# A shared ring of four SBUF slots split into two of two, and one product of the down projection read out by ACT

## The chip, the cores and the metric

The kernel runs on one core of a Trainium2 chip. Its engines are TensorE (PE, matrix products), VectorE (DVE), ScalarE (ACT), GpSimd (POOL) and SyncE (SP, which here issues most of the DMAs); each works through its own instructions in order and waits on semaphores for the others. SBUF is the working memory on the chip, PSUM receives PE's products. The metric is the device time of one execution in microseconds, as the median of the runs. Times in the trace are microseconds from the start of the span, durations marked ns are nanoseconds.

## What is computed

One layer of a post-norm trunk over 1024 positions of width 1024, in float32. A layer norm is followed by one input projection that feeds three mixers, an output projection, a norm, a gated feed-forward part with a gated input embedding, and a last norm:

```python
h = layer_norm(x, ln_in_g, ln_in_b)
proj = h @ w_in
a_q, a_f, a_i, a_g, b_u, b_v, c_q, c_kv, c_kr = split(proj)
o_a = hgrn2_mixer(a_q, a_f, a_i, a_g, ...)   # gated linear recurrence, 4 heads of 64
o_b = sgu_mixer(b_u, b_v, ...)               # causal gating in chunks of 128
o_c = mla_mixer(c_q, c_kv, c_kr, cos, sin, ...)   # causal attention, 8 heads, low-rank q and kv
mix = concatenate([o_a, o_b, o_c]) @ w_out
h = layer_norm(ALPHA * h + mix, ln1_g, ln1_b)
gate, up = split(h @ w_gate_up)
ffn = (silu(gate) * up) @ w_down             # D_FF = 2816
ple = sigmoid(h @ ple_w_gate) * (p @ ple_w_proj)
h = layer_norm(ALPHA * h + ffn + ple, ln2_g, ln2_b)
```

## The kernel before

Rows of positions lie in 8 tiles of 128. The projections take each float32 operand as a high and a low part and add three products (high by high, low by high, high by low), so one product of a 128-row tile with a weight of 1024 rows is 24 matmuls: `cq` 384 columns wide, `gb` 512, `ck` 288. In the trace a plain float32 matmul leaves two records.

The stages follow one another in time, by the trace: layer norm, embedding product and the value and gate projections of the recurrence (`vg`, products ai) to about 94 us; its forget and query projections (af, aq) to 138; the recurrence's scores in levels, to about 205; its chunk states (kE, kv); the low-rank query products (cq); from 237 the outputs of the recurrence (`ho`) and the gating unit (gb, uv, z), until 318; the key and value products (ck), the transposes ct and the q and k projections to 393; attention to 545; output projection, norm, embedding gate (pgt); the gate and up products from 725 to 1148; the down products to 1376; the last norm to the end.

**The recurrence's levels** (L420 to L447): the scores S of the recurrence are built in seven levels of two halves. For each half PE makes the products `lv` (L430) from q and k, DVE copies the masked part into S (L434) and multiplies q and k by the decay for the next level (L440, L443), which the next `lv` needs. Then, for four pairs of tiles (tp), a tile `vk` with the values is loaded from HBM (L464, L465), PE transposes k (kE, L470), ACT copies it (L473), PE makes kv from it and vk (L478), ACT copies that into kvs (L482), and DVE adds the states up (L485).

**cq** (L489 to L499): for each of the 8 tiles PE makes the product into a PSUM ring of two, ACT squares it into a tile `cn` (L495) to get the sum, POOL takes the inverse root (L140, L141), ACT scales the product into `cn` (L498), and SP stores `cn` to HBM (L499). ck (L565 to L574) does the same with its 8 tiles (L569, L572, L574). Later `cnl` loads them back, and PE transposes them (ct).

**ho** (L514 to L538): for each tp the values `vo` and gates `go` are loaded (L516, L518), PE makes the products of S with vo and of kvs with q into one PSUM tile (the only one of its ring), ACT squares it with sums (L533), POOL takes the inverse roots, DVE multiplies (L537, which is the last read of the PSUM tile) and multiplies by go (L538). The result is transposed (mx) and stored to `mix_d` (L458). The gating unit (L541 to L556) has its spatial weights and norm rows in a tile `sgp`, loaded at L503 to L507.

**gate and up** are Strassen-like products, seven of half-sized operands in place of eight; sums and differences of weights (`s`, on POOL at L1031 and elsewhere; `wp`, `st` on DVE at L110 and ACT at L790) are the operands. The last lines of such a product (L1008 to L1019) read the PSUM tiles.

**down** (L1093 to L1125) goes in two halves of chunks of the feed-forward width; `Down(i, ...)` holds the state of one block of rows i (0 to 3), and `product(m)` makes the seven products m. Their PSUM tiles dY, dZ, dW are opened by some m and reused by others with more terms; after each product its sum so far is added into the result tile r. Products 1, 7 and 6 go through an ACT copy into a tile `cp` (L1122) and a POOL add (L1123); the others are added by DVE straight from PSUM (L1125). In the last chunk the final norm of each row block runs beside the products (L1135 to L1157, L162, L163).

**Slots.** Every small tile comes from a ring with a fixed number of slots; a tile waits until the one that had its slot has been read for the last time. `ld` gives tiles of 128 x 512 words or less from the ring "X" with 4 slots, and `sm` is the same function under another name. From it come, in order of the program: vg (L277), the masks cmf and mski, `vk`, `cn` of cq, triu, vo and go, `cn` of ck, perm, the operands mixh and mixl, hx and sg at the embedding gate (L924, L935), g and s in gate, up and down (L1008, L1017, L1030), and four of every seven `cp`.

What sets the order on each engine is a scheduler: the program is written stage by stage, and the tile framework simulates it with its own durations and emits each engine's instructions in the order in which they came up there (`schedule_with_timeline_sim=True`). That order is then fixed: an engine never passes a waiting instruction. The number of slots of a ring thus changes the order on all engines.

Of the kernel before, what the change touches and what calls it, by code (L numbers as in the profile page):

```python
# [9 lines left out]
F32 = mybir.dt.float32  # L10
F32R = mybir.dt.float32r
# [3 lines left out]
ALU = mybir.AluOpType  # L15
AX = mybir.AxisListType

P = 128
# [25 lines left out]
def build(tc, A, out):  # L44
    nc = tc.nc
    ctx = ExitStack()
    with ctx:
# [9 lines left out]
        def nm(s):  # L57
            uid[0] += 1
            return f"{s}_{uid[0]}"
# [17 lines left out]
        smH = smt("smH", 3)  # L77

        def ld(shape, dt=F32, n="ld"):
            return xp.tile(list(shape), dt, tag="X", name=nm(n), bufs=4)  # L80

        sm = ld

        def ti(tag, w=8, bufs=4):
            return cp.tile([P, w], F32, tag="ti" + tag, name=nm("ti" + tag), bufs=bufs)
# [18 lines left out]
        V = nc.vector  # L104
# [597 lines left out]
        def mix_first():  # L702
            r = []
            for u in range(2):
                hi = ld([P, 4, P], F32R, n="mixh")
                lo = ld([P, 4, P], F32R, n="mixl")
                mr = lo.bitcast(F32)
                dma(out=mr, in_=mix_d[0][0][:, 4 * u:4 * u + 4])
                nc.scalar.copy(out=hi, in_=mr)
                sub_lo(V, lo, mr, hi)  # L710
                r.append((hi, lo))
            return [[r[k // 4][a][:, k % 4] for k in range(NK)] for a in range(2)]
# [94 lines left out]
        class Block:  # L807


            def __init__(self, n, new=None):  # L810
                self.t = [[(new or hb_tile)([P, 2, 512], n) for _ in range(2)] for _ in range(2)]
# [106 lines left out]
        for hf in range(2):  # L918
            wq = [wpage(A["w_pg"][hf * 4 + u]) for u in range(4)]
            cs = slice(hf * 512, hf * 512 + 512)  # L920
            for t in ((0, 1, 2, 3, 4, 5, 6, 7), (4, 5, 6, 7, 0, 1, 2, 3))[hf]:
                pl = t2("cp", 3, "pl")
                dma(out=pl, in_=pl_d[t][:, cs])
                hx = ld([P, 512], n="hx")  # L924
                dma(out=hx, in_=h1_d[t][:, cs])
                ps = ps_("ZYW"[n % 3], "pgt")
                c = slice((t % 4) * P, (t % 4 + 1) * P)
                for k in range(NK):
                    b = HB[k // 4, t // 4]
                    wh = wq[k // 2][0][:, (k % 2) * 512:(k % 2) * 512 + 512]  # L930
                    wl = wq[k // 2][1][:, (k % 2) * 512:(k % 2) * 512 + 512]
                    mm(ps, b.at(0, k % 4, c), wh, start=(k == 0), stop=False)  # L932
                    mm(ps, b.at(0, k % 4, c), wl, start=False, stop=False)  # L933
                    mm(ps, b.at(1, k % 4, c), wh, start=False, stop=(k == NK - 1))  # L934
                sg = ld([P, 512], n="sg")  # L935
                act(out=sg, in_=ps, func=AF.Sigmoid)
                V.tensor_tensor(out=sg, in0=pl, in1=sg, op=ALU.mult)
                V.scalar_tensor_tensor(out=sg, in0=hx, scalar=ALPHA, in1=sg, op0=ALU.mult, op1=ALU.add)
                dma(out=r_d[t][:, cs], in_=sg)
                n += 1  # L940
                if n in (3, 5, 11, 13):
                    sums_of_h((n - 3) // 2 if n < 9 else (n - 7) // 2)
# [78 lines left out]
        def down_operands(j, x0, x1):  # L1021

            a11, a21, a12, a22 = x0[:, :512], x0[:, 512:], x1[:, :512], x1[:, 512:]
            s = {1: a11, 2: a12, 4: a22}

            def step(m, in0=None, in1=None, how=None):
                def run():
                    if in0 is not None:
                        a, b = (s[q] if isinstance(q, int) else q for q in (in0, in1))
                        s[m] = ld([P, 512], n="s")  # L1030
                        G.tensor_tensor(out=s[m], in0=a, in1=b, op=how)  # L1031
                    st = (hb_tile([P, 2, 2, 256], "st") if j == NF // 2 - 1 else
                          gu.tile([P, 2, 2, 256], F32R, tag="st", name=nm("st"), bufs=2))
                    sv = s[m].rearrange("p (q n) -> p q n", q=2)
                    split(st[:, :, 0, :], st[:, :, 1, :], sv)
                    sdma(out=a_d[j][m].rearrange("q p a n -> p q a n"), in_=st.bitcast(F32))
                return run

            return [step(5, a21, a22, ALU.add), step(1), step(6, 5, a11, ALU.subtract), step(2),
                    step(3, a12, 6, ALU.subtract), step(4), step(7, a11, a21, ALU.subtract)]  # L1040
# [49 lines left out]
            return dn.tile([P, 512], F32, tag=tag, name=nm(n or tag), bufs=bufs)  # L1090

        class Down:
            def __init__(self, i, at, bt, opens):  # L1093
                self.i, self.at, self.bt, self.ps, self.opens = i, at, bt, {}, opens
                for t in (i, i + 4):
                    if r_t[t] is None:
                        r_t[t] = dn.tile([P, D], F32, tag="r", name=nm("r"), bufs=NT)

            def product(self, m):
                bank = BANK[m]  # L1100
                if m in OPENS:
                    self.ps[bank] = pd.tile([P, 512], F32, tag=bank, name=nm("d" + bank), bufs=DBUFS[bank])
                o = self.ps[bank]
                cs = slice((self.i % 2) * P, (self.i % 2 + 1) * P)
                a = self.at[self.i // 2][m]
                n = len(self.bt)
                for k in range(n):
                    b = self.bt[k][m]
                    mm(o, a[:, k, 0, cs], b[:, 0, :], start=(m in OPENS and k == 0), stop=False, skip_group_check=True)  # L1109
                    mm(o, a[:, k, 0, cs], b[:, 1, :], start=False, stop=False, skip_group_check=True)  # L1110
                    mm(o, a[:, k, 1, cs], b[:, 0, :], start=False, stop=(k == n - 1), skip_group_check=True)  # L1111
                r0, r1 = r_t[self.i], r_t[self.i + 4]
                r = {1: r0[:, :512], 2: r0[:, :512], 7: r1[:, 512:], 6: r1[:, :512], 4: r1[:, :512],
                     5: r1[:, 512:], 3: r0[:, 512:]}[m]
                if self.opens and m in (1, 7, 6):
                    nc.scalar.copy(out=r, in_=o)
                elif self.opens and m == 3:
                    V.tensor_copy(out=r, in_=o)
                elif m in (1, 7, 6):
                    nw[1] += 1  # L1120
                    c = ld([P, 512], n="cp") if nw[1] % 7 < 4 else d2("cp", 3)
                    nc.scalar.copy(out=c, in_=o)  # L1122
                    G.tensor_tensor(out=r, in0=r, in1=c, op=ALU.add)  # L1123
                else:
                    V.tensor_tensor(out=r, in0=r, in1=o, op=ALU.add)  # L1125

# [40 lines left out]
        for ci, js in enumerate(CHUNKS):  # L1167
# [19 lines left out]
                    dma(out=raw, in_=A["ln2"][u:u + 1, :].partition_broadcast(P))  # L1187
                    ln2.append(raw)
            for pair in ([(0, 1), (2,), (3,)] if last else [(0, 1), (2, 3)]):
                pair = [Down(i, at, bt, ci == 0) for i in pair]  # L1190
                for d in pair:
                    d.product(1)
                if pending:
# [101 lines left out]
```

## Time and profile before

| | us |
|---|---|
| median of 3 runs | 1397.91 (1396.21 to 1401.93) |
| profiled execution | 1394.26 |
| its span | 1392.5 |
| PE busy | 1313.4 (94%) |
| DVE busy | 937.2 (67%) |
| ACT busy | 593.4 (43%) |
| POOL busy | 572.6 (41%) |

The span runs from the first to the last instruction; 1.76 us of the profiled execution lie around it. An engine's busy time is an average over stages. PE is near its full span, so the stages where it is not are the ones to look at, by the table of busy time in stretches. In the timelines, the bracket at the end of a row gives the idle time of the engine just before the row, and the instruction that ended it. The mean granted clock of PE over the execution is 0.984.

### The profile page before, as it was taken

The numbers are of one execution on the slowest core, as the hardware profiler recorded it, in microseconds if no ns is written. First come the engines' busy times: TensorE is split into PE (matmuls) and PEld (weight loads), VectorE is DVE, ScalarE is ACT, GpSimd is POOL, SyncE is SP. The second block draws the span as 40 slices with busy tenths as digits, with TensorE's granted clock in tenths as the row PEclk, the third lists the DMA queues.
The fourth block names the chain that finished last, engine by engine and source line by source line (L and its number), as shares of the span: only waits on it lengthen the run. The fifth ranks groups of instructions, "written<-read, shape, count | busy, mean of one in ns | idle before, by whom it ended". The sixth has DMA issues, their size and how long they took to land.

```text
span 1392.5 us, 18446 instructions
## 1 busy us (share of the span) xinstructions
PE 1313.4 (94%) x6484; PEld 1097.4 (79%) x6484; DVE 937.2 (67%) x1357; ACT 593.4 (43%) x1189; POOL 572.6 (41%) x475
## 2 busy tenths in 40 slices
PE   6999779999989998999999999999999998999993
PEld 4788669898768887888888788888888876887882
DVE  7842691344567776676765787777777778577658
ACT  5543004335267775245434444444444445333441
POOL 3220002221223332323533554445544445899657
PEclk9999999999989999999999999999999999999997
DMA  9741002235595534447951444434434478996723
GB/s 328 260 137 46 31 1 90 90 96 160 157 336 121 113 72 150 163 179 262 314 191 61 165 159 148 145 139 145 157 137 152 166 265 308 393 316 228 258 61 121
DMA packets 105324, 237.52 MB, mean 171 GB/s; under 512 B 11152, under 2 KB 22416, under 8 KB 103696
## 3 DMA queue, kind: packets, MB, share of 16 engines
q1 hardware_dynamic: 84288, 195.97, 42.6%
q10 hardware_dynamic: 20944, 40.38, 7.7%
q8 instruction: 51, 0.84, 0.3%
q14 instruction: 41, 0.34, 0.1%
HBM read 150.98 MB, written 85.33 MB: 170 GB/s over the span
## 4 chain that ended last, share of the span: by engine, by line
PE 75%; DVE 9%; DMA 5%; POOL 4%; ACT 3%; issue 3%; SPq 0%; ACTq 0%; DVEq 0%; POOLq 0%
PE Y L1000 5%; PE Y L1001 5%; PE Y L999 5%; PE W L999 2%; PE W L1000 2%; PE W L1001 2%; PE pgt L934 2%; PE pgt L933 2%; PE pgt L932 2%; PE op L871 2%; PE pt L756 2%; PE op L869 2%; PE op L870 2%; POOL r L1123 2%; PE dY L1109 2%
## 5 line engine op out<-in xcount | busy, mean ns | idle before, releaser
L110 DVE TENSOR_TENSOR wp<-s,wp 128x512 fp32r<-128x512 f32 x132 | 145.2, 1108 | 46.6 <-ACT wp L790 46.1
L790 ACT CAST wp<-s 128x512 fp32r<-128x512 f32 x132 | 80.6, 621 | 86.9 <-POOL s L969 25.7
L110 DVE TENSOR_TENSOR wp<-raw,wp 128x512 fp32r<-128x512 f32 x99 | 100.5, 1020 | 6.9 <-ACT wp L790 6.7
L790 ACT CAST wp<-raw 128x512 fp32r<-128x512 f32 x99 | 60.5, 622 | 86.9 <-PE Y L1001 42.0
L1123 POOL TENSOR_TENSOR r<-r,cp 128x512 f32<-128x512 f32 x60 | 86.3, 1460 | 15.2 <-ACT cp L1122 15.2
L750 POOL TENSOR_SCALAR P<-P,tiar 128x384 f32<-128x384 f32 (+3 forms) x64 | 47.9, 750 | 102.7 <-DVE tiar L749 83.3
L965 POOL TENSOR_TENSOR s<-raw,s 128x512 f32<-128x512 f32 x22 | 32.6, 1481 | 129.3 <-DVE wp L110 129.3
L1109 PE MATMUL dY<-wp,A 128*128 128x512 f32 x176 | 68.7, 396 | 7.0 <-DVE r L1125 6.4
L999 PE MATMUL Y<-T,wp 128*128 128x512 f32 x176 | 68.6, 390 | 1.5 <-ACT cp L1005 1.5
L999 PE MATMUL Y<-B,wp 128*128 128x512 f32 x176 | 68.6, 390 | 1.3 <-DVE x L1015 1.3
L1110 PE MATMUL dY<-wp,A 128*128 128x512 f32 x176 | 69.2, 393 | 0.5 <-DVE wp L110 0.5
L999 PE MATMUL W<-T,wp 128*128 128x512 f32 x176 | 68.6, 390 | 0.8 <-ACT cp L1005 0.8
L1111 PE MATMUL dY<-wp,A 128*128 128x512 f32 x176 | 68.9, 393 | 0.0
L1000 PE MATMUL W<-T,wp 128*128 128x512 f32 x176 | 68.5, 389 | 0.0
L1001 PE MATMUL Y<-B,wp 128*128 128x512 f32 x176 | 68.5, 389 | 0.0
L1000 PE MATMUL Y<-T,wp 128*128 128x512 f32 x176 | 68.5, 389 | 0.0
L1000 PE MATMUL Y<-B,wp 128*128 128x512 f32 x176 | 68.5, 389 | 0.0
L1001 PE MATMUL W<-T,wp 128*128 128x512 f32 x176 | 68.5, 389 | 0.0
L1001 PE MATMUL Y<-T,wp 128*128 128x512 f32 x176 | 68.5, 389 | 0.0
L110 DVE TENSOR_TENSOR st<-s,st 128x512 fp32r<-128x512 f32 x44 | 56.5, 1284 | 12.1 <-ACT st L790 10.4
L110 DVE TENSOR_TENSOR wlo<-raw,whi 128x1024 fp32r<-128x1024 f32 (+3 forms) x27 | 32.8, 1223 | 43.9 <-ACT whi L122 43.5
L762 DVE TENSOR_TENSOR PTl<-pt,PTh 128x512 fp32r<-128x512 f32 (+2 forms) x96 | 51.3, 547 | 12.3 <-ACT PTh L761 12.2
(363 smaller groups left out, 4084.7 us busy)
## 6 DMA issues: line engine op xcount, KB each, us to landing
a_d<-st ACTq DMA_DIRECT2D x77, 512.0 KB, 2.8
A<-a_d SPq DMA_DIRECT2D x154, 256.0 KB, 5.3
raw<-in_w_gu_dram SPq DMA_DIRECT2D x44, 512.0 KB, 3.6
raw<-in_w_dn_dram SPq DMA_DIRECT2D x22, 512.0 KB, 4.1
x<-in_x_dram SPq DMA_DIRECT2D x8, 512.0 KB, 6.3
h_d<-x SPq DMA_DIRECT2D x8, 512.0 KB, 4.8
pl_d<-plo SPq DMA_DIRECT2D x16, 256.0 KB, 5.1
raw<-in_w_out_dram SPq DMA_DIRECT2D x8, 512.0 KB, 6.8
```

The source lines that it names most:

```text
L110: eng.tensor_tensor(out=lo, in0=src, in1=hi, op=ALU.subtract)
L750: G.tensor_scalar(out=pr[:, :n], in0=pr[:, :n], scalar1=rc, scalar2=1.0, op0=ALU.mult, op1=ALU.mult)
L762: V.tensor_tensor(out=PTl[:, j0:j1, c * P:(c + 1) * P], in0=src, in1=dh, op=ALU.subtract)
L790: nc.scalar.copy(out=hi, in_=src)
L965: G.tensor_tensor(out=s4, in0=a12, in1=s2, op=ALU.subtract)
L999: mm(o, w[:, 0, ks], b.at(0, k), start=(m in OPENS and k == 0), stop=False, skip_group_check=True)
L1000: mm(o, w[:, 0, ks], b.at(1, k), start=False, stop=False, skip_group_check=True)
L1001: mm(o, w[:, 1, ks], b.at(0, k), start=False, stop=(k == 3), skip_group_check=True)
L1109: mm(o, a[:, k, 0, cs], b[:, 0, :], start=(m in OPENS and k == 0), stop=False, skip_group_check=True)
L1110: mm(o, a[:, k, 0, cs], b[:, 1, :], start=False, stop=False, skip_group_check=True)
L1111: mm(o, a[:, k, 1, cs], b[:, 0, :], start=False, stop=(k == n - 1), skip_group_check=True)
L1123: G.tensor_tensor(out=r, in0=r, in1=c, op=ALU.add)
```

## The change

The ring X has two slots in place of four, and `sm` has a ring of its own, XM, with two. `ld` keeps vk, vo, go, perm, the first half of mixh and mixl, hx, g and some cp; `sm` has vg, the masks, cn, triu, the second half of mixh and mixl, sg, s and the other cp. Of the copies cp, four of seven still come from these rings. In the last chunk, product 5 of each of the four row blocks is copied out of PSUM by ACT (L1122 of before, one line further down in the changed kernel), and DVE adds the copy.

```diff
         def ld(shape, dt=F32, n="ld"):
-            return xp.tile(list(shape), dt, tag="X", name=nm(n), bufs=4)
-
-        sm = ld
+            return xp.tile(list(shape), dt, tag="X", name=nm(n), bufs=2)
+
+        def sm(shape, dt=F32, n="sm"):
+            return xp.tile(list(shape), dt, tag="XM", name=nm(n), bufs=2)
...
-                hi = ld([P, 4, P], F32R, n="mixh")
-                lo = ld([P, 4, P], F32R, n="mixl")
+                hi = (ld, sm)[u]([P, 4, P], F32R, n="mixh")
+                lo = (ld, sm)[u]([P, 4, P], F32R, n="mixl")
...
-                sg = ld([P, 512], n="sg")
+                sg = sm([P, 512], n="sg")
...
-                        s[m] = ld([P, 512], n="s")
+                        s[m] = sm([P, 512], n="s")
...
-                elif m in (1, 7, 6):
+                elif m in (1, 7, 6) or (self.last and m == 5):
                     nw[1] += 1
-                    c = ld([P, 512], n="cp") if nw[1] % 7 < 4 else d2("cp", 3)
+                    c = (ld if nw[1] % 7 < 2 else sm)([P, 512], n="cp") if nw[1] % 7 < 4 else d2("cp", 3)
                     nc.scalar.copy(out=c, in_=o)
-                    G.tensor_tensor(out=r, in0=r, in1=c, op=ALU.add)
+                    (V if m == 5 else G).tensor_tensor(out=r, in0=r, in1=c, op=ALU.add)
```

`Down` gets a further argument `last`, true in the last chunk. Lines from L84 on are one further down in the changed kernel.

Since the slots set the order, instructions move on all engines. Three places are shown, as the kernels have them. A name's first number counts the tiles.

PE, at the first levels of the recurrence. Before:

```order
L406 MATMUL dg_193_1129<-q_177_981,k_166_860 128x256
L406 MATMUL dg_193_1129<-q_182_1043,k_172_921 128x256
L406 MATMUL dg_193_1129<-q_177_981,k_166_860 128x256
L406 MATMUL dg_193_1129<-q_182_1043,k_172_921 128x256
L430 MATMUL lv_196_1141<-q_177_981,k_166_860 128x128
L430 MATMUL lv_197_1157<-q_177_981,k_166_860 128x128
L430 MATMUL lv_196_1141<-q_182_1043,k_172_921 128x128
L430 MATMUL lv_196_1141<-q_177_981,k_166_860 128x128
L430 MATMUL lv_196_1141<-q_182_1043,k_172_921 128x128
L430 MATMUL lv_196_1141<-q_177_981,k_166_860 128x128
L430 MATMUL lv_196_1141<-q_182_1043,k_172_921 128x128
L430 MATMUL lv_196_1141<-q_177_981,k_166_860 128x128
```

The changed kernel, at the same lv products (cq_248 is the fourth of the eight cq products):

```order
L248 MATMUL cq_248_1562<-whi_228_1444,hTlo_62_152 128x384
L246 MATMUL cq_248_1562<-whi_228_1444,hThi_60_150 128x384
L431 MATMUL lv_196_1141<-q_177_981,k_166_860 128x128
L247 MATMUL cq_248_1562<-wlo_229_1445,hThi_60_150 128x384
L248 MATMUL cq_248_1562<-whi_228_1444,hTlo_62_152 128x384
L246 MATMUL cq_248_1562<-whi_231_1450,hThi_60_150 128x384
L247 MATMUL cq_248_1562<-wlo_232_1451,hThi_60_150 128x384
L248 MATMUL cq_248_1562<-whi_231_1450,hTlo_62_152 128x384
L431 MATMUL lv_197_1157<-q_177_981,k_166_860 128x128
L246 MATMUL cq_248_1562<-whi_231_1450,hThi_60_150 128x384
L247 MATMUL cq_248_1562<-wlo_232_1451,hThi_60_150 128x384
L248 MATMUL cq_248_1562<-whi_231_1450,hTlo_62_152 128x384
```

The cq products from the third on, which stood behind the kE and kv products, now stand between and ahead of the lv products; six of them, and the first gb products, lie ahead of the first kE.

ACT, behind the query projection (aq). Before:

```order
L392 ACTIVATE q_177_981<-aq_178_984 64x512 x4
L122 CAST whi_267_1733<-raw_266_1731 128x1024
L392 ACTIVATE q_182_1043<-aq_183_1046 64x512 x4
L473 COPY kE_213_1373<-kE_212_1368 128x512
L482 COPY kvs_210_1365<-kv_214_1375 64x256 x2
L495 ACTIVATE cn_240_1491,tic_241_1492<-cq_239_1466 128x384
L473 COPY kE_217_1389<-kE_216_1384 128x512
L498 ACTIVATE cn_240_1491<-cq_239_1466,tic_241_1492 128x384
```

The changed kernel:

```order
L393 ACTIVATE q_177_981<-aq_178_984 64x512 x4
L123 CAST whi_267_1733<-raw_266_1731 128x1024
L393 ACTIVATE q_182_1043<-aq_183_1046 64x512 x4
L496 ACTIVATE cn_240_1491,tic_241_1492<-cq_239_1466 128x384
L499 ACTIVATE cn_240_1491<-cq_239_1466,tic_241_1492 128x384
L496 ACTIVATE cn_243_1523,tic_244_1524<-cq_242_1498 128x384
L499 ACTIVATE cn_243_1523<-cq_242_1498,tic_244_1524 128x384
L496 ACTIVATE cn_246_1555,tic_247_1556<-cq_245_1530 128x384
```

The copies of kE and kv no longer stand ahead of the first reads of cq; all eight cn tiles and three uv tiles come before the first kE copy.

SP, from the loads of the weights of ck to those of vo and go. Before:

```order
L116 DMA raw_362_2327<-in_w_ck_dram 128x864
L509 DMA triu_264_1726<-in_triu_dram 128x128
L516 DMA vo_278_1755<-v_d_17_90 128x512
L518 DMA go_279_1757<-g_d_21_94 128x512
L116 DMA raw_365_2333<-in_w_ck_dram 128x864
L116 DMA raw_368_2339<-in_w_ck_dram 128x576
L116 DMA raw_419_2765<-in_w_ukv_dram 128x1024
L516 DMA vo_299_1895<-v_d_18_91 128x512
L499 DMA cn_d_32_105<-cn_261_1715 128x384
L518 DMA go_300_1897<-g_d_22_95 128x512
L516 DMA vo_320_2039<-v_d_19_92 128x512
L518 DMA go_321_2041<-g_d_23_96 128x512
```

The changed kernel, from behind the first vo load to the third:

```order
L117 DMA raw_422_2771<-in_w_ukv_dram 128x1024
L117 DMA raw_425_2777<-in_w_uq_dram 128x768
L519 DMA go_279_1757<-g_d_21_94 128x512
L459 DMA mix_d_33_106<-m_312_1986 128x256
L117 DMA raw_428_2783<-in_w_uq_dram 128x768
L517 DMA vo_299_1895<-v_d_18_91 128x512
L117 DMA raw_431_2789<-in_w_uq_dram 128x768
L459 DMA mix_d_33_106<-m_319_2036 128x256
L519 DMA go_300_1897<-g_d_22_95 128x512
L575 DMA cn_d_25_98<-cn_372_2370 128x288
L588 DMA cnl_403_2621<-cn_d_25_98 128x672
L517 DMA vo_320_2039<-v_d_19_92 128x512
```

The loads of vo and go stood close together, ahead of the stores to mix_d; now these stores and weight loads lie between them, and vo_320 stands behind go_300, the first ck store (cn_372) and its reload cnl_403. Further up, not shown, the loads vk_219 and vk_223 have moved from between the loads of the cq weights to behind the stores of cq, and the loads of sgp follow vk_219.

In the same stretch PE had all eight gb products around the four ho products before, with ck behind; in the changed kernel all gb products lie ahead of the first ho product, and 24, 46 and 26 ck matmuls stand between the first and second, second and third, and third and fourth ho product.

## Rows read from the trace of the kernel before

**Rows 1.** The page, section 1: busy us (share of the span) xinstructions of each engine.

```profile
PE 1313.4 (94%) x6484; PEld 1097.4 (79%) x6484; DVE 937.2 (67%) x1357; ACT 593.4 (43%) x1189; POOL 572.6 (41%) x475
```

**Rows 2.** Busy time by stretch: stretch, length, each engine's busy us, PE clock, DMA share, GB/s.

```profile
151.20:209.80 58.60, 40.97 (x257) 35.07 (x257) 51.59 (x76) 3.07 (x7) 0.74 (x2) 0.91 0.03 10
...
800.00:1100.00 300.00, 300.00 (x1326) 248.47 (x1325) 233.56 (x248) 135.81 (x247) 145.12 (x96) 1.00 0.44 154
1140.00:1170.00 30.00, 22.20 (x87) 16.29 (x87) 28.03 (x34) 17.32 (x34) 17.08 (x11) 0.97 0.70 242
1352.80:1389.10 36.30, 17.48 (x69) 13.20 (x68) 34.84 (x48) 10.20 (x17) 31.28 (x26) 0.83 0.27 101
```

**Rows 3.** Groups of PE in 151.2 to 209.8: busy, mean ns | idle before <-releasers.

```profile
L430 PE MATMUL lv<-q,k 128*128 128x128 f32 x224 | 35.7, 312 | 14.9 <-DVE q L443 7.2 <-DVE S L434 5.4 <-DVE q L415 1.5
```

**Rows 4.** Tile cn (min/median/max ns, first to last start us); then a wait of ACT.

```profile
L495 ACT ACTIVATE cn<-cq x8: 491/492/495, 207.5 to 237.8; 128x384 f32<-128x384 f32 x8
...
ACT kE L473 <- PE kE L470: 63.9, 1, 63.9
```

**Rows 5.** Tile vk: the kv products on PE and the loads on SP.

```profile
L478 PE MATMUL kv<-vk,kE x32: 272/275/377, 205.5 to 229.1; 128*128 128x128 f32 x32
L465 SPq DMA_DIRECT2D vk<-v_d x4: 320/346/430, 94.8 to 102.0; - x4
```

**Rows 6.** Timeline of PE: start us, us, line, operation [idle before <-releaser].

```profile
156.24 3.44 PE L430 MATMUL lv<-q,k 128*128 128x128 f32 x28 [0.64 <-DVE q L415]
...
210.06 0.34 PE L246 MATMUL cq<-wlo,hThi 128*128 128x384 f32 x1
...
213.88 0.34 PE L247 MATMUL cq<-whi,hTlo 128*128 128x384 f32 x1
...
237.53 0.39 PE L245 MATMUL gb<-whi,hThi 128*128 128x512 f32 x1
...
240.07 0.39 PE L247 MATMUL gb<-whi,hTlo 128*128 128x512 f32 x1
```

**Rows 7.** Timeline of ACT, then of DVE, behind the first ho product.

```profile
244.70 0.23 ACT L533 ACTIVATE os<-ho 128x64 f32<-128x64 f32 x1 [0.69 <-PE ho L527]
...
249.49 0.68 DVE L537 TENSOR_TENSOR os<-ho,tih 128x512 f32<-128x512 f32 x1
...
250.69 0.69 DVE L538 TENSOR_TENSOR os<-os,go 128x512 f32<-128x512 f32 x1
```

**Rows 8.** Timeline of PE in the first ck product.

```profile
304.11 0.29 PE L246 MATMUL ck<-wlo,hThi 128*128 128x288 f32 x1
...
306.37 0.30 PE L245 MATMUL ck<-whi,hThi 128*128 128x288 f32 x1
```

**Rows 9.** Tile vo: landing time of its four loads.

```profile
DMA to landing us min/median/max: 2.7/3.0/5.7
```

**Rows 10.** Tile vg: ACT's copies into it.

```profile
L278 ACT COPY vg<-ai x8: 351/373/395, 37.9 to 93.5; 128x256 f32<-128x256 f32 x8
```

**Rows 11.** Timeline of PE where the down products begin.

```profile
1157.14 0.50 PE L1109 MATMUL dZ<-wp,A 128*128 128x512 f32 x1 [1.41 <-DVE r L1125]
...
1167.01 0.50 PE L1109 MATMUL dW<-wp,A 128*128 128x512 f32 x1 [3.24 <-DVE r L1125]
```

**Rows 12.** Groups of ACT in 1340 to 1390: the copies out of PSUM.

```profile
L1122 ACT COPY cp<-dY 128x512 f32<-128x512 f32 x6 | 3.4, 588 | 5.0 <-PE dY L1111 5.0
```

**Rows 13.** Timeline of PE at its end, then one row of DVE.

```profile
1367.12 0.50 PE L1109 MATMUL dY<-wp,A 128*128 128x512 f32 x1 [2.78 <-DVE r L1125]
...
1373.41 0.79 PE L1109 MATMUL dY<-wp,A 128*128 128x512 f32 x1 [3.27 <-DVE r L1125]
...
1375.71 0.63 PE L1111 MATMUL dY<-wp,A 128*128 128x512 f32 x1
...
1368.82 0.69 DVE L1125 TENSOR_TENSOR r<-r,dY 128x512 f32<-128x512 f32 x1 [1.15 <-PE dY L1111]
```

**Rows 14.** Line 1019: a DVE add of two SBUF tiles, min/median/max ns.

```profile
L1019 DVE TENSOR_TENSOR x<-x,g x22: 674/692/1462, 752.2 to 1150.7; 128x512 f32<-128x512 f32 x22
```


## What the change will do to the time

> **What bounds the kernel now.** I read the share of each engine first. TensorE (PE) is busy 1313.4 us of a span of 1392.5 [rows 1], so 79 us are left in which it stands, and a change that shortens anything but PE's path counts only in those. Next comes the table of busy time by stretch [rows 2]. From 800 to 1100 us, inside the gate and up products, PE is busy 300.00 of 300.00: whatever the split ring does to the order of the small sums there, nothing on PE can be gained, and a delay shows only if it uses up PE's stock of finished operands. Two places have idle PE that this change touches, and one holds most of it: from 151.2 to 209.8, the levels of the recurrence, PE is busy 40.97 of 58.60 us and its mean granted clock is 0.91, so part of the stretch ran at the lower of its two levels (1.2 and 2.4 GHz). DVE is busy 51.59 there. The groups of that stretch say who PE waits for: 224 lv products, with 14.9 us idle before them, released by the DVE steps q and S [rows 3]. The levels are a chain PE, DVE, PE, DVE, and PE has nothing else to do.
>
> It could have something. Directly behind the levels stand 6 of the 8 cq products, which need only h and weights. They are not there earlier because their results have no slot. ACT reads a cq product into a tile cn, and the first such read is at 207.5 [rows 4]. In ACT's order the kE copy stands ahead of it, and there ACT waits 63.9 us. The four vk tiles are loaded from 94.8 on, but are read only by the kv products, which run from 205.5 to 229.1 [rows 5]: they hold all four slots of the ring X through the levels. Two cq products fit into PSUM; the other six cannot start.
>
> **The split ring, in the levels.** With vk in X and cn in a ring of its own, the new order lets ACT read cn directly after q, with no kE copy between, and PE gets cq products between the lv groups (first two places of the order). I count 6 cq products and all but two matmuls of 3 gb products ahead of the first kE. A cq product is 24 matmuls; from 210.06 to 213.88 there are 22 steps of 0.174 us [rows 6], so 4.2 us each, 25 us in all. A gb product is 24 steps of 0.23 (from 237.53 to 240.07 are 11 steps, [rows 6]), 5.5 us. Fill available: 25 + 16 = 41 us.
>
> What is there to fill: at the full clock 28 lv records took 3.44 us [rows 6] (an f32 product leaves two records); less 0.27, the length of a single one (as in [rows 5]), 27 steps of 0.117. The stretch holds 257 records, nearly all of this kind [rows 2], that is 30.1 us of work in 58.6. So 28.5 us are lost, 17.6 as idle time and about 11 to the lower clock and to the tails of short bursts. The fill is larger, so PE should be busy throughout, and DVE, at 51.59 us plus three weight subtractions that move in, should fit under the 30 + 41 = 71 us of PE. Upper bound of this term: 28.5 us; nearest lower bound 0 (rival 3).
>
> **What is late next.** The work that moves forward was cover for what follows it. In the new order the four ho products have ck products between them, where gb products stood before. A ho tile leaves PSUM only after a chain: ACT reads it from 244.70 (0.69 us after the product's end at 244.01), and when POOL has taken the roots, DVE multiplies from 249.49 to 250.17 [rows 7]: 6.2 us from the end of the product, and 7.4 to the end of the next DVE step, which frees the go tile (251.38). ho has one PSUM buffer. A ck product is 24 steps of 0.133 us (17 steps from 304.11 to 306.37, [rows 8]), 3.2 us. Between the first and second ho stand 24 ck matmuls and some small ones, about 3.7 us, so PE waits 2.5; between the second and third 46, about 6.6, no wait; between the third and fourth 26, about 4.2, a wait of 2. That is 4.5 us. The ring of two also puts the loads of vo and go one behind the other on SP, each waiting for a release, with the mix_d stores of the other products and the cn stores behind them (third place of the order). A vo load lands 2.7 to 5.7 us after its issue [rows 9], and the first has about 6 us of gb and kE work as cover: 0 to 2 us, and I take 1. The weights sgp of the gating unit now stand on SP behind vk_219, which waits for the first kv product; some 37 gb matmuls (8.5 us) lie ahead of the first user: I take 1 of 0 to 2. Net of the front: 28.5 - 4.5 - 2 = 22 us gained. The mask load mski moves four places back on SP; its masks are first used in the levels, after 151.2, behind 44 us of other PE work, so nothing. The eight vg tiles of the input phase get two slots instead of a share of four; they are written over some 56 us [rows 10], 8 us apart on average, so nothing as well; the price if two come close together is one store's landing.
>
> **Gate, up and the change to down.** The sums s get slots of their own and are issued earlier or later by a place. PE's 300.00 of 300.00 hides that; without this cover each would cost at most its wait. From 1140 to 1170 PE is busy 22.20 of 30.00 [rows 2], and two of its waits are for a DVE read of a down product: 1.41 and 3.24 us [rows 11]. In the new order DVE does such reads ahead of two of the subtractions that stood before them. Ends: 0 and -4.65 us; I take -1.5, since the subtractions are put off, not gone, and PE's next operands come from them.
>
> **The fifth product of the last chunk.** It swaps a DVE add that reads PSUM for an ACT copy (four of 0.59 us, [rows 12]) and a DVE add that reads two SBUF tiles: DVE's count of adds is the same. What it frees is PSUM: PE waited 2.78 and 3.27 us for DVE to read this product [rows 13]. But after that DVE is the end: from 1352.8 on it is busy 34.84 of 36.30 us [rows 2], while PE is done at 1376.3 [rows 13]. DVE's own wait for PE there is 1.15 us [rows 13], and that is all that earlier products can give. Against it stands the add itself: the SBUF add of the same shape, x<-x,g, took 0.674 at least, 0.692 as the median and 1.462 at most [rows 14]; four times 0.79 more is 3.2 us. Ends -1.15 and +3.2. Two of the four adds fall into those last 36 us, where POOL is busy 31.28; if both are long they cost 1.6, and some of the 1.15 comes back: I take +1.
>
> The Trainium skill, "SBUF — State Buffer", section "Who interferes with whom", says that a DVE instruction with two SBUF inputs contends with a GpSimd instruction that reads SBUF, whereas with one SBUF input it does not. The row agrees, 0.69 and 1.46 us for one and the same add, and it speaks against this edit: with all four adds long the sum would be 2.2 us more, with none 1.6 less.
>
> **Sum.** The profiled execution took 1394.26 us (span 1392.5 and 1.76 around it). 1394.26 - 22 - 1.5 + 1 = 1371.8. The median of the runs shown, 1397.91, is 1.0026 times the profiled time, so 1375 us.
>
> **The rivals.**
> 1. **The hgrn outputs become the bound.** If gb and ck work drifts ahead of the ho products, as PE runs in order and other waits shift it, the last three ho products wait their 6.2 us in full: 18.6 instead of 4.5. For it: little cover is left by the order. Against it: ck cannot run ahead, its place is fixed. 1371.8 + 14.1 = 1385.9, as a median 1389.
> 2. **Slower: SP's queue with rings of two.** In the new order the load vo of the third group stands behind go of the second, which waits for the first group's go tile. A group is then a ho product of 30 records at lv's step, 3.5 us, 7.4 to free its go tile, and a load of up to 5.7: 16.6 us. If nothing overlaps between groups, four take 66.4 us, with 25.6 of ck and 14 of ho for PE to do: 26.8 of standing. With 5.7 for the first vo load and 3.2 of stretched adds in the tail that is 35.7 against 28.5 gained: 1394.26 + 7.2 = 1401.5, as a median 1405, and more where the cn stores held behind those loads make attention late. It decides from some 35 us of new idle PE. For it: SP is in order and one blocked load holds the stores behind it. Against it: vo of the next head needs only the ho product, not the go release.
> 3. **The fill hides nothing.** An lv group now stands behind cq matmuls on PE, so DVE waits for it; if each level simply becomes longer by its fill, the 41 us are only moved and the kernel stays at about 1397. For it: PE's order is fixed, and DVE's chain of 51.59 us is the longest there. Against it: the fill lies between the groups of the two halves, so DVE has the one while PE does the other.
>
> **Chances.** Forecast 0.72 (1364 to 1382), rival 1 0.16 (1382 to 1392), rival 3 0.08, rival 2 0.04. A measurement tells about 0.5% of this kernel from no change, so the bounds are 1390.9 and 1404.9: faster 0.87 (the forecast and nearly all of rival 1), same 0.08, slower 0.05. The low end is the sum of all favourable ends: 1394.26 - 28.5 - 4.65 - 1.15 = 1360, as a median 1364. The high end, 1390, takes in rival 1 at its full price.
>
> **What would show it.** Right: no cn wait at kE on ACT, cq matmuls from 152 us on, PE busy nearly all of the levels at a clock of 1.00, the first kE some 10 us later than now, and attention beginning about 20 us earlier. The ho products would show waits on the DVE multiply of about 2 us, twice. Wrong: idle PE of over 10 us between the first kE and the q projections (rival 1 or 2), SP issues of go with long gaps (rival 2), or DVE idle time in the levels as large as the fill (rival 3). In the last 36 us I expect DVE busy nearly all the time, with the four adds at 0.69 or at 1.46 us, and PE's waits of 2.78 and 3.27 gone.

## The result, and the profile after

The changed kernel takes 1366.25 us (median; 1365.02 to 1368.49), the kernel before in the same comparison 1398.68. The ratio is 0.977, 95% interval [0.974, 0.979]. Two further comparisons gave 0.978 [0.976, 0.980] and 0.979 [0.977, 0.981]. The profiled execution of the changed kernel took 1365.61 us, its span is 1363.8: 28.65 us less than the profiled execution before. The prediction was 1375, so the sign, the place and the range (1364 to 1382) held, the range near its low end, and the gain was larger than forecast: 28.65 by the profiles, where my sum had 22.5.

The levels answer first. These are rows of the table of busy time by stretch of the changed kernel (stretch, length, busy us of PE, PEld, DVE, ACT, POOL, PE clock, DMA share, GB/s): the same stretch as in [rows 2], then the two others named there, moved to where they now lie.

```profile
151.20:209.80 58.60, 58.60 (x390) 56.55 (x389) 47.87 (x64) 13.77 (x27) 9.33 (x17) 1.00 0.17 55
1112.00:1142.00 30.00, 23.44 (x90) 17.69 (x90) 26.68 (x34) 17.31 (x33) 17.44 (x12) 0.94 0.75 250
1324.10:1360.40 36.30, 17.13 (x66) 12.49 (x64) 35.99 (x48) 12.00 (x22) 31.98 (x27) 0.74 0.27 101
```

PE is busy 58.60 of 58.60 us at a granted clock of 1.00, where it was 40.97 at 0.91. The group of lv in 151.2 to 219 and the row of cn say the same from the two sides:

```profile
L431 PE MATMUL lv<-q,k 128*128 128x128 f32 x224 | 27.9, 275 | 0.0
```
```profile
L496 ACT ACTIVATE cn<-cq x8: 482/492/493, 142.5 to 193.2; 128x384 f32<-128x384 f32 x8
```

The 224 lv records take 27.9 us and have no idle time before them; in [rows 3] they took 35.7 with 14.9 idle. ACT reads the first cq product at 142.5 and the last at 193.2, in [rows 4] it began at 207.5. The first kE product is at 219.1, 15.6 us later than before, since the levels now carry the cq work.

How far the gain lasts is read from the first instruction of each later stage. Here is the first row of attention (sc) and of the down products (dY), before and then after (min/median/max ns, first to last start us):

```profile
L736 PE MATMUL sc<-qk x96: 273/392/794, 393.4 to 529.6; 96*128 96x512 f32 x40, 96*128 96x384 f32 x16, 96*128 96x256 f32 x16, 96*128 96x320 f32 x16
```
```profile
L1109 PE MATMUL dY<-wp,A x176: 389/389/794, 1148.2 to 1374.9; 128*128 128x512 f32 x176
```
```profile
L737 PE MATMUL sc<-qk x96: 272/392/793, 366.1 to 502.1; 96*128 96x512 f32 x40, 96*128 96x384 f32 x16, 96*128 96x256 f32 x16, 96*128 96x320 f32 x16
```
```profile
L1110 PE MATMUL dY<-wp,A x176: 388/389/792, 1120.2 to 1344.4; 128*128 128x512 f32 x176
```

Attention begins 27.3 us earlier (393.4 to 366.1), down 28.0 (1148.2 to 1120.2), the last dY product 30.5 (1374.9 to 1344.4). The span ends 28.7 earlier. So the front holds nearly everything; PE gains another 2.5 in the down products, and the end gives back 1.8 of it. The 2.5 is not steady: from its first to its last dY product PE took 226.7 us before and 224.2 here, but 226.5 when the changed kernel was run for the third time (below).

What the front gained is of two kinds. Up to the beginning of attention PE leaves nearly the same number of records in both kernels, 1921 and 1920 (before, then after; columns as above):

```profile
0.00:393.40 393.40, 358.41 (x1921) 306.74 (x1922) 213.52 (x389) 139.58 (x315) 73.16 (x102) 0.98 0.40 134
```
```profile
0.00:366.10 366.10, 349.44 (x1920) 302.32 (x1921) 214.28 (x389) 140.03 (x315) 72.23 (x102) 1.00 0.43 144
```

PE's idle time fell from 35.0 to 16.7 us, so by 18.3, and its busy time by 9.0, of which the lv records have 7.8, while the granted clock rose from 0.98 to 1.00.

Behind the levels, where I feared the ho products, the waits of PE from 138 to 400 us are (engine, line, released by: us in total, times, longest):

```profile
PE sc L737 <- ACT P L748: 5.2, 3, 4.4
PE v L639 <- ACT ckT L601: 2.3, 2, 1.8
PE v L641 <- DVE ckT L604: 0.5, 1, 0.5
PE kE L471 <- ACT kvs L483: 0.4, 1, 0.4
...
PE ho L525 <- DVE os L538: 0.2, 1, 0.2
```

The wait at ho is 0.2 us. The wait of 2.8 at v takes the place of the 3.1 that PE waited at ct before, and that of sc was there before as well.

At the start of down, and at the end (timelines: start us, us, engine, line, operation [idle before <-releaser]):

```profile
1130.24 0.80 PE L1110 MATMUL dZ<-wp,A 128*128 128x512 f32 x1 [2.50 <-DVE r L1126]
...
1140.46 0.50 PE L1110 MATMUL dY<-wp,A 128*128 128x512 f32 x1 [0.87 <-DVE r L1126]
...
1142.66 0.50 PE L1110 MATMUL dW<-wp,A 128*128 128x512 f32 x1 [1.23 <-ACT r L1117]
```
```profile
1332.80 0.50 PE L1110 MATMUL dY<-wp,A 128*128 128x512 f32 x1 [0.67 <-ACT cp L1123]
...
1340.51 0.50 PE L1110 MATMUL dY<-wp,A 128*128 128x512 f32 x1 [3.32 <-ACT cp L1123]
...
1342.98 0.79 PE L1110 MATMUL dY<-wp,A 128*128 128x512 f32 x1 [0.68 <-ACT cp L1123]
```
```profile
1336.52 1.68 DVE L1124 TENSOR_TENSOR r<-r,cp 128x512 f32<-128x512 f32 x1
...
1346.09 0.68 DVE L1124 TENSOR_TENSOR r<-r,cp 128x512 f32<-128x512 f32 x1
```
```profile
1336.37 2.96 POOL L1124 TENSOR_TENSOR r<-r,cp 128x512 f32<-128x512 f32 x2
```

Compared with [rows 11], PE still waits, partly at other products: with the smaller waits on either side, 7.3 us from the last gate and up products on, 8.3 before (8.9 the third time). At the end PE's waits of 2.78 and 3.27 us for DVE [rows 13] have become 0.67, 3.32 and 0.68 for the ACT copy. PE ends 30.4 us earlier, but DVE is busy 35.99 of its last 36.30 us, as it was [rows 2]. Two of the four SBUF adds lie in that stretch: the one at 1336.52 runs beside a POOL add and takes 1.68 us, the one at 1346.09 takes 0.68.

### The profile page after: what moved, and what is told of

The parts are those of the page before. It is cut to its first block, busy times and chain, and to the rows that moved or that the text cites. A ratio compares the mean times of both kernels' runs of the same rounds, so it can differ in the third digit from the quotient of the medians.

```text
span 1363.8 us, 18478 instructions
## 1 busy us (share of the span) xinstructions
PE 1304.0 (96%) x6484; PEld 1093.0 (80%) x6484; DVE 936.6 (69%) x1357; ACT 596.6 (44%) x1193; POOL 568.5 (42%) x475
## 5 line engine op out<-in xcount | busy, mean ns | idle before, releaser
L111 DVE TENSOR_TENSOR wp<-s,wp 128x512 fp32r<-128x512 f32 x132 | 132.6, 1017 | 46.2 <-ACT wp L791 45.9
L111 DVE TENSOR_TENSOR wp<-raw,wp 128x512 fp32r<-128x512 f32 x99 | 90.3, 917 | 8.2 <-ACT wp L791 8.2
L963 POOL TENSOR_TENSOR s<-raw 128x512 f32<-128x512 f32 x22 | 30.3, 1377 | 86.0 <-DMA raw<-in_w_gu_dram 77.7
L791 ACT CAST st<-s 128x512 fp32r<-128x512 f32 x44 | 27.4, 622 | 73.2 <-POOL s L1032 30.4
```

The lines of the kernel that those rows point to most:

```text
L111: eng.tensor_tensor(out=lo, in0=src, in1=hi, op=ALU.subtract)
L791: nc.scalar.copy(out=hi, in_=src)
L963: G.tensor_tensor(out=s1, in0=a21, in1=a22, op=ALU.add)
```

## The experiments

Ratios are to the kernel before, run beside each kernel on the same chip, with their 95% intervals.

| kernel | ratio | attention begins at, us |
|---|---|---|
| changed, second and third time | 0.9779 [0.9764, 0.9795], 0.9790 [0.9772, 0.9808] | 365.7, 366.6 |
| split only | 0.9781 [0.9766, 0.9795] | 365.1 |
| product 5 only | 1.0003 [0.9990, 1.0015] | 394.6 |
| split, cn of cq in X | 1.0028 [1.0013, 1.0043] | 396.1 |
| before, cn of cq in another ring | 0.9816 [0.9801, 0.9831] | 369.4 |
| before, vk in a ring of two, X of two | 1.0054 [1.0034, 1.0075] | 376.7 |
| before, one slot for cn, X of three | 0.9837 [0.9822, 0.9851] | 368.5 |
| changed, product 5 added by POOL | 0.9791 [0.9776, 0.9806] | 365.8 |
| changed, statistics of tile 7 on ACT | 0.9793 [0.9774, 0.9812] | 366.2 |
| changed, statistics of tiles 2 and 7 on ACT | 0.9786 [0.9769, 0.9803] | 366.2 |

**The two halves apart.** The changed kernel was run again beside a kernel with the rings alone and one with the readout alone.

> The changed kernel again, beside the two halves of the change. Both theories: ratio to the kernel before 0.977, about 1366 us.

Split only:

```diff
-                elif m in (1, 7, 6) or (self.last and m == 5):
+                elif m in (1, 7, 6):
```

> The two rings without the new readout of product 5. Theory A (the whole gain is cn getting slots while vk waits for the levels): attention starts at about 366 us as in the changed kernel, ratio 0.976 to 0.979, so within 2 us of the changed kernel; PE has its two waits for DVE near the end again (2.8 and 3.3 us) at no cost, since DVE ends the kernel. Theory B (the new readout brings part of the gain, the 6 us of PE waits near the end): ratio 0.980 or more, 1370 us or later.

Product 5 only: the kernel before with the last two pieces of the change (the condition, and the add on DVE for m == 5).

> The new readout of product 5 with one ring of four slots. Theory A: ratio 0.998 to 1.002, levels as before (PE idle about 17.6 us), attention starts at 393 us. Theory B: ratio 0.995 to 0.997, some 4 to 6 us less than before.

The rings alone give 0.9781, the whole change 0.9779, the readout alone 1.0003. Theory B falls: PE's waits near the end are worth nothing that these runs can measure. They are there in the split kernel (its PE, timeline):

```profile
1339.37 0.50 PE L1110 MATMUL dY<-wp,A 128*128 128x512 f32 x1 [2.78 <-DVE r L1126]
...
1346.88 0.80 PE L1110 MATMUL dY<-wp,A 128*128 128x512 f32 x1 [2.90 <-DVE r L1126]
```

and its span still ends within 1.6 us of the changed kernel's. In the kernel with the readout alone the four adds are (min/median/max ns):

```profile
L1123 DVE TENSOR_TENSOR r<-r,cp x4: 679/693/1683, 1351.0 to 1379.6; 128x512 f32<-128x512 f32 x4
```

**Is it cn?** The split kernel with one line taken back:

```diff
-            cn = sm([P, 384], n="cn")
+            cn = ld([P, 384], n="cn")
```

> The changed kernel, but the cn tiles of the cq products come from ring X again, with its two slots, where the four vk tiles stand ahead of them. Theory A: the first cn read waits for the kv products again, PE idles 17 us or more in the levels at a clock below 1.00, attention starts at 390 to 397 us, ratio 0.995 to 1.003. Theory B (the gain in the front comes from another user of the rings, vg, the masks, vo, go or the cn of ck): attention starts before 380 us, ratio 0.977 to 0.990.

The whole gain is gone, and 0.3% more. Its levels by the table of stretches, and its cn:

```profile
151.20:209.80 58.60, 40.19 (x251) 33.76 (x249) 51.83 (x76) 1.62 (x4) 0.00 (x0) 0.91 0.01 4
```
```profile
L496 ACT ACTIVATE cn<-cq x8: 486/492/492, 215.4 to 243.0; 128x384 f32<-128x384 f32 x8
```

PE is busy 40.19 of 58.60 at a clock of 0.91, and ACT reads the first cq product at 215.4: the picture of before. With X of two, the third and fourth vk tiles must first get the slots of the first two, and cn stands behind them, so it comes 8 us later than with four slots.

**Is it only cn?** The same from the other side, the kernel before with one edit; smS is the ring of uv, which nothing used in the levels of the kernel before, and ring X keeps four slots for all others:

```diff
-            cn = sm([P, 384], n="cn")
+            cn = smS([P, 384], n="cn")
```

> The kernel before with a single edit: the cn tiles of cq come from another ring of four (that of uv, idle at that time); ring X keeps four slots, all other tiles stay, product 5 as before. Theory A (only that cn has no slot while vk waits): PE busy over 57 of the 58.6 us from 151.2, attention starts at 364 to 368 us, ratio 0.975 to 0.980. Theory B (the split's other users count too): ratio 0.984 or more.

PE is busy 58.60 of 58.60 in the levels, but attention begins at 369.4, later than the 364 to 368 of theory A, and the ratio, 0.9816, lies between the two theories. Its waits of PE behind the levels, 205 to 370 us:

```profile
PE ct L591 <- DVE ckT L603: 3.1, 1, 3.1
PE mx L454 <- DVE uv L553: 1.0, 1, 1.0
PE ct L591 <- ACT kraw L601: 0.9, 1, 0.9
```

These are 5.0 us at ct and mx, where the changed kernel has 2.8 at v. Down begins at 1127.0, 6.8 us behind the changed kernel. So cn alone brings 24.0 of the 27.3 us at the front. The rest, and some 3 us more up to the down products, is by subtraction what the other tiles gain by the split. Which of them does was not separated, nor what cn in their ring costs the uv tiles.

**Does any split do?** Four slots in all, but cut in another place: vk alone in a ring of two, everything else in X with two.

```diff
-            return xp.tile(list(shape), dt, tag="X", name=nm(n), bufs=4)
+            return xp.tile(list(shape), dt, tag="X", name=nm(n), bufs=2)
...
-            vv = ld([P, 2, 256], n="vk")
+            vv = xp.tile([P, 2, 256], F32, tag="XV", name=nm("vk"), bufs=2)
```

> The kernel before with four slots in all, but vk alone in a ring of two and everything else sharing a ring X of two. Theory A: the front as in the changed kernel, attention at 364 to 370 us; gate and up stay covered (PE 300 of 300), so ratio 0.975 to 0.982. Theory B (s and sg need slots apart from g and hx): PE shows waits from 700 to 1120 us and the ratio is 0.985 or more.

It is 0.5% slower than before, which neither theory had. Theory B named one part of it, PE's waits in gate and up. The levels are filled as in the changed kernel, but behind them PE stands; two stretches, then the longest of its waits in the output projection, in attention, and in gate and up:

```profile
151.20:209.80 58.60, 58.60 (x391) 56.51 (x390) 47.88 (x64) 13.77 (x27) 9.33 (x17) 1.00 0.18 59
270.00:300.00 30.00, 25.87 (x154) 24.72 (x153) 6.74 (x20) 8.54 (x47) 7.71 (x12) 0.72 0.28 90
```
```profile
PE op L869 <- ACT mixh L709: 11.8, 1, 11.8
...
PE sc L736 <- ACT P L747: 7.0, 9, 4.4
...
PE W L999 <- ACT cp L1005: 6.6, 2, 4.5
```

From 270 to 300 PE is busy 25.87 of 30 us at a mean clock of 0.72, and attention begins at 376.7, 10.6 us later than in the changed kernel; the waits of PE in between are at many places, none over 2.2 us in all. The output projection waits 11.8 us for mixh: its first operands take four tiles at once, a high and a low part for two halves, and X has two; the second pair was cast at 540.9 us. In the changed kernel the halves come from different rings. Gate and up lose as well: down begins at 1158.6. Theory A was right on the levels and wrong on the rest: slots must also be apart for tiles that are alive together.

**How many slots does cn need?** One, with three for the others:

```diff
-            return xp.tile(list(shape), dt, tag="X", name=nm(n), bufs=4)
+            return xp.tile(list(shape), dt, tag="X", name=nm(n), bufs=3)
...
-            cn = sm([P, 384], n="cn")
+            cn = xp.tile([P, 384], F32, tag="XC", name=nm("cn"), bufs=1)
```

> The kernel before with three slots in X and one slot that only the cn tiles of cq use. A cn tile is held for about 4.5 us (ACT 0.68, POOL about 1.3, ACT 0.58, store 1.9), a cq product takes PE 4.2 us and more with the lv products between. Theory A (it is who holds the slots, not how many there are): attention at 364 to 370 us, ratio 0.975 to 0.983. Theory B (the number of slots for cn sets the gain): about half the gain, attention at 375 us or later, ratio 0.986 or more.

At the front theory A holds: with one slot, attention begins at 368.5, 24.9 of the 27.3 us. The ratio, 0.9837, is just past its bound, and by the trace the loss lies later, with three slots for the rest: down begins at 1128.9, 8.7 us behind the changed kernel, with waits such as this one in gate and up.

```profile
PE W L999 <- ACT cp L1005: 3.0, 1, 3.0
```

**What bounds the end?** The add of product 5 on POOL, in the changed kernel:

```diff
-                    (V if m == 5 else G).tensor_tensor(out=r, in0=r, in1=c, op=ALU.add)
+                    G.tensor_tensor(out=r, in0=r, in1=c, op=ALU.add)
```

> The changed kernel with the add of the copied product 5 on POOL instead of DVE. It takes four adds (0.68 to 1.68 us) from DVE, which ends the kernel, and gives POOL four adds of 1.3 to 1.75. Theory A (DVE alone bounds the last 36 us): up to 2 us less than the changed kernel, ratio 0.975 to 0.978. Theory B (POOL, busy 32 of those 36 us, bounds it as well, directly or by stretching the DVE instructions beside it): the same or up to 4 us more, ratio 0.978 to 0.981.

The ratio, 0.9791, is within the intervals of the changed kernel; the median, 1370.0, is 2 to 4 us above its medians, but the kernel before was slower beside it as well (1399.6, and 1397.2 to 1398.7 in the other comparisons). So the 2 us of theory A did not come. PE ends about where it did, and DVE's norm steps became longer. The first of them, in the 36.6 us that end 3.4 before the span's end, with POOL adding and then in the changed kernel (group: busy, mean ns | idle before):

```profile
L163 DVE SCALAR_TENSOR_TENSOR r<-r,til,ln 128x512 f32<-128x512 f32 x9 | 12.8, 1455 | 0.0
```
```profile
L163 DVE SCALAR_TENSOR_TENSOR r<-r,til,ln 128x512 f32<-128x512 f32 x10 | 11.0, 1142 | 0.0
```

A step takes 1455 ns in place of 1142. Over the last 100 us, where both kernels have all 20 norm steps, these take 27.3 us in place of 23.5, and the four adds that left DVE had taken 3.7 in all: what DVE was spared it lost again. That speaks for theory B. To see it from DVE's side, the changed kernel was run with less work on DVE: the statistics of row tile 7, then of 2 as well, on ACT (`act` with a running sum, as the code does for tiles 4, 5 and 6).

```diff
-            if t in (4, 5, 6):
+            if t in (4, 5, 6, 7):
```

> The changed kernel beside the next two: 1366 to 1368 us, ratio 0.977 to 0.978.

> The changed kernel with the norm statistics of row tile 7 on ACT in place of DVE (two bn_stats, aggregate and one small step, 1.7 us less on DVE; ACT gets 2.6 us, of which it has plenty near the end). Theory A (DVE's queue alone sets the last 20 us): 1 to 2 us less than the changed kernel. Theory B (the chain of the last row tile or POOL sets it): no difference, within 0.7 us.

> The same with row tile 2 as well: DVE has 3.4 us less. Theory A: 2 to 3.5 us less than the changed kernel, ratio 0.975 to 0.976. Theory B: no difference or longer, since the statistics of tile 2 then stand in ACT's queue ahead of the copies that free PSUM for PE.

The three give 0.9790, 0.9793 and 0.9786: no difference that can be told. The traces show where the work went. From the second of the four product 5 adds to DVE's last step, in the changed kernel, with one tile moved and with two (stretches; then, for two tiles, the one wait of DVE that is new):

```profile
1322.50:1360.50 38.00, 18.73 (x73) 13.82 (x71) 37.57 (x50) 13.56 (x24) 33.45 (x28) 0.75 0.26 97
```
```profile
1324.03:1361.75 37.72, 19.60 (x73) 14.39 (x71) 37.36 (x46) 16.05 (x29) 34.93 (x29) 0.74 0.25 92
```
```profile
1326.09:1363.40 37.31, 18.56 (x73) 13.81 (x71) 35.10 (x42) 18.20 (x34) 34.61 (x30) 0.83 0.26 98
```
```profile
1347.36 1.59 DVE L1124 TENSOR_TENSOR r<-r,cp 128x512 f32<-128x512 f32 x1 [1.89 <-ACT cp L1123]
```

With one tile moved, 1.7 us of steps are gone and no wait came in, yet the stretch is 0.3 us shorter and DVE's busy time 0.2: the 20 norm steps took 24.7 us in place of 23.5. With two, 3.4 us are gone and the stretch is 0.7 us shorter: DVE's busy time fell by 2.5, but it now waits 1.89 us for a copy cp that stands behind the statistics in ACT's queue, as theory B had it.

That DVE's steps stretch because POOL runs beside them fits the two adds shown above (0.68 and 1.68 us) and the run with the POOL adds. It also fits one and the same pair of norm steps in the changed kernel, first while POOL stood idle, then beside its adds (DVE, then POOL):

```profile
1349.20 1.40 DVE L164 SCALAR_TENSOR_TENSOR r<-r,til,ln 128x512 f32<-128x512 f32 x2
...
1353.34 3.45 DVE L164 SCALAR_TENSOR_TENSOR r<-r,til,ln 128x512 f32<-128x512 f32 x2
```
```profile
1350.98 0.99 POOL L1147 TENSOR_TENSOR til<-til,mhalf 128x1 f32<-128x1 f32 x1 [2.28 <-DVE til L1146]
...
1354.53 3.38 POOL L1158 TENSOR_TENSOR r<-r,ln 128x512 f32<-128x512 f32 x2
```

But no run took POOL's work away, so how far POOL bounds the last 20 us beside DVE stays open.

## Why the prediction was right, and where its sum was off

**The place and the cause: right.** cn had no slot while vk waited for the levels. Taking cn out of the ring of vk gives the gain, putting it back takes all of it away.

**The size of the lost time: right.** I worked out 28.5 us lost in the levels as the upper bound, from 257 records at 0.117 us. The front gained 27.3, and its parts agree as well: 18.3 of idle and 9.0 of busy time, where I had 17.6 and about 11.

**What is late next: wrong, and most of the difference.** I took 4.5 us back for waits of the ho products and 2 for the loads of vo and sgp. Measured: 0.2 at ho, none at z or for vo. The failed step is the chain of 6.2 us from the end of a ho product to the end of the DVE multiply. In the changed kernel (ACT, POOL, DVE, then PE):

```profile
259.38 0.23 ACT L534 ACTIVATE os<-ho 128x64 f32<-128x64 f32 x1 [1.25 <-PE ho L528]
```
```profile
261.49 1.65 POOL L142 TENSOR_TENSOR tih<-tih,mhalf 128x8 f32<-128x8 f32 x1
```
```profile
263.18 0.69 DVE L538 TENSOR_TENSOR os<-ho,tih 128x512 f32<-128x512 f32 x1 [2.04 <-POOL tih L142]
```
```profile
263.92 0.43 PE L525 MATMUL ho<-vo,S 128*128 128x64 f32 x2 [0.24 <-DVE os L538]
```

From ACT's first read to the end of the DVE multiply it takes 4.5 us. I had made two errors in reading [rows 7]. These rows of the kernel before show them (PE, POOL, DVE):

```profile
244.28 0.39 PE L527 MATMUL ho<-kvs,q 128*128 128x64 f32 x2
```
```profile
246.82 1.65 POOL L141 TENSOR_TENSOR tih<-tih,mhalf 128x8 f32<-128x8 f32 x1
```
```profile
249.09 0.48 DVE L162 SCALAR_TENSOR_TENSOR uv<-uv,tig,sgp 128x256 f32<-128x256 f32 x1
```

The 0.69 in the bracket of ACT's row is ACT's own idle time, which began when ACT had finished its step before; it does not say that the product ended 0.69 us ahead of the read. The product ended at 244.67, 0.03 us ahead. And between the roots (done at 248.47) and the multiply (249.49), DVE was busy with the norm of the gating unit, work of its queue at that moment and no part of the chain. The two make up the 1.7 us. The cover was a little longer than I took it as well: 4.3 us of z, ck and mx products from ACT's read on, where I had 3.7. Against a chain of 4.5 the wait is the 0.24 of the last row, and between the third and fourth ho product, where I had 2 us, there is none. The sgp weights did come late, as expected, but for POOL and DVE, not for PE:

```profile
  DMA sgp<-in_wsT_dram: 4.5, 1
  DMA sgp<-in_rows_dram: 3.3, 1
```

**The start of down: within its ends.** Taken -1.5, measured 7.3 for 8.3 us of waits, so -0.9; with 8.9 us the third time, the sign is not settled.

**Product 5: near enough in the sum, not in every part.** Taken +1, ends -1.15 and +3.2. The readout alone moved the time by 0.0003 of it, 0.4 us, with an interval of 1.7 to either side, so it cannot be told from 0 or from +1. PE's waits, which I expected gone, stayed for the most part: 4.7 us for ACT's copies, where 6.05 us for DVE had been. DVE was the last to work, as the row of 34.84 of 36.30 us had said. But I counted only its wait of 1.15 for PE; another ended just where that stretch begins, and in the changed kernel a wait for the copy stands there (before, then after):

```profile
1352.82 0.69 DVE L1125 TENSOR_TENSOR r<-r,dY 128x512 f32<-128x512 f32 x1 [1.80 <-PE dY L1111]
```
```profile
1322.52 0.69 DVE L1124 TENSOR_TENSOR r<-r,cp 128x512 f32<-128x512 f32 x1 [1.91 <-ACT cp L1123]
```

Of the two adds in the last 36 us one was long, 1.0 us more than before in all; I had put 1.6. The Trainium skill, "SBUF — State Buffer", section "Who interferes with whom", says that a DVE instruction with two SBUF inputs contends with a GpSimd instruction that reads SBUF. The trace agrees for the add at 1336.52, 1.68 us beside a POOL add of SBUF tiles that had begun at 1336.37; the add at 1346.09, beside which POOL has only steps of 128x1, took 0.68.

**The scale to the median.** I multiplied by 1.0026, since the profiled execution before was 3.65 us under its median. The changed kernel's profiled execution was 0.6 under its own. That is 3.0 of the 3.8 us by which the difference of the medians (32.4) exceeds that of the profiles (28.65); the other 0.8 is the median before, 1398.68 in this comparison and 1397.91 when I predicted. So this part is which execution was profiled, not the change.

**The rivals.** Rival 1 did not occur (0.2 us of waits for 18.6), nor rival 3: the levels became longer by their fill, the first kE 15.6 us later, but the fill was then missing behind them, so PE's idle time shrank. What rival 2 describes, rings of two whose users wait for each other, was seen in the kernel with vk alone in its ring: the price was some 38 us against the changed kernel (0.0275 of 1398), 10.6 of them at the front, but little of that at ho (1.2 us of waits), where rival 2 had it; 11.8 stood at mixh, and most of the rest in gate and up.

## What to carry to other kernels

Where an engine idles on a chain between two others, look for independent work that stands directly behind it and ask what keeps it there; here it was not an engine but a slot, and the row that told it was a load issued some 110 us ahead of its use. For a short-lived tile, a ring shared with long-lived ones is only as large as what they leave free: split it by how long the tiles live, and keep tiles that are needed at once in different rings, since the wrong split of the same four slots lost the whole gain again. And when the time of a chain is read from a trace, take the bracket as idle time of the waiting engine only, and leave out what else stood in the queues.

## What was not expected

One slot for cn gave 24.9 of the 27.3 us at the front: a tile held for under 5 us need not have two. The same count of slots, four, gave 0.977 with one cut and 1.005 with another. Taking 3.4 us of work from the engine that is busy to the end changed nothing that can be measured: 2.5 of it left DVE's busy time, while 1.9 us of a new wait for ACT's copy came in.
